# A hybrid attention and gMLP layer: the last gates are projected first, and q, k and the gMLP's constants take their pool

## The chip, the cores and the metric

The kernel runs on one core of one Trainium2 chip. The core has TensorE (PE, matrix products, with weight loads of its own, PEld), VectorE (DVE), ScalarE (ACT), GpSimd (POOL) and SyncE (SP), whose queue issues every transfer of this kernel. The metric is device time in microseconds of one execution; a time is the median of several runs. A profiled execution gives the trace from which the rows come; times in it count from the first instruction.

## What is computed

One decoder layer on 2048 tokens of width 1024, 8 heads of 64, a gMLP of width 512 in 4 groups, in float32 to the accuracy of the reference:

```python
a = _rmsnorm(h, g_in[i])
z = jnp.einsum('bsd,de->bse', a, w_in[i])
q, k, v, gate_b, u_a, v_a, gate_a = jnp.split(z, ...)          # seven groups of 512 columns
q = _rope(_rmsnorm(q, q_norm[i]), positions); k = _rope(_rmsnorm(k, k_norm[i]), positions)
o_b = _dilated_attention(q, k, v) * jax.nn.silu(gate_b)         # windows (128,1), (512,4), (2048,16)
o_a = _gmlp_spatial(u_a, v_a, w_spatial[i], b_spatial[i], ...) * jax.nn.silu(gate_a)
h = h + jnp.einsum('bse,ed->bsd', jnp.concatenate([o_b, o_a], axis=-1), w_out[i])
gate = jax.nn.sigmoid(jnp.einsum('bsd,de->bse', _rmsnorm(h, g_ple[i]), w_ple_gate[i]) + b_ple_gate[i])
h = h + gate * jnp.einsum('bsp,pd->bsd', p[i], w_ple_proj[i])
```

Each of the three dilated branches is causal attention of a query over 128 keys back at its stride; the branches are merged with weights in proportion to their softmax denominators. `_gmlp_spatial` is `gelu(u)` times a lower-triangular 128x128 mix of `LN(gelu(v))` in each chunk of 128 tokens.

## The kernel before

Tokens go in 16 tiles of 128. Every product of the layer is made of three float32r products of split operands (hi x hi, hi x lo, lo x hi; `project`, line 222, and `gm_product`, line 614): 24 matmuls of 512 columns. A group of 512 columns of weights is loaded in eight pieces of 256 KB into staging buffers (`stage()`, line 239, a pool of four), cast by ScalarE to the hi half (line 132), and VectorE or GpSimd subtracts for the lo half (line 134). It lies in a slot; three slots (`ring`) are used in turn, and the gate's group has one of its own in the pool `p1g`.

The work has three stages.

*Projection* (lines 268 to 539). For each tile the normalised row block is turned (`prep`), and four products g, q, k, v are made (`step`). q and k get norm and rotary embedding, are split into f16 halves, turned by a transposing transfer and stored (`d_qk`); v goes to `d_v` in two orders of tokens, the gate to `d_gb`. Everything on SP is in order. The last two tiles, 14 and 15, are done at the end, in the written order of PE (`manual_schedule`, line 529): q14 q15 k14 k15 v14 v15, then g14 g15 (lines 532 to 539). The pool `p1` is closed ahead of the gates, and the pool `pg` opens there, into which `gm_constants` (line 455) loads five constants of the gMLP, `bs` among them. `spatial_weights` (line 464) masks and turns the spatial matrices and scales `bs`; it is called in the first gate product of the gMLP (line 655).

*Attention and gMLP* (lines 598 to 841). Heads go in four pairs; a pair has three branches (0, 2, 1) of four quads of query tiles. A step (`Step`) makes scores for one or two tiles of both heads. `scores` (line 739): PE multiplies, VectorE adds the mask and takes the negated maximum into `o` (line 750), ScalarE takes the exponential (line 755). `turn` (line 758), one step later: ScalarE scales by 2^14 (line 762), VectorE casts to f16 (line 763), GpSimd subtracts for the lo half (line 113), and SP issues a transposing transfer (line 767; line 771 for narrow steps) out of a staging buffer of the pool of four. `values` (line 773), six steps after the scores: PE multiplies the turned tile with v (line 781), VectorE copies (line 787), and a finished quad of `o` is stored to `d_o` (line 790). There are 152 steps. Between them, `fill` puts gMLP products of the first 13 tiles into PE's written order, `FILL` = 1.3 us after each step and `BLOCK0` = 18 us ahead of the first; `gmlp` counts 0.43 us for two matmuls. The gMLP's own chain is the same for each tile: `gm_v`, `gm_u`, `gm_g`, GELU in `gelu2` (line 604), products in the two banks `mm`. q and k of a head pair lie in `qk`, and the next pair's are loaded in four chunks of 512 tokens over the last two quads of a pair and the first two of the next (`load_qk`, line 256, and lines 824 to 828), six transfers each; `load_v` (line 718) loads values two quads ahead.

*Output* (lines 844 to 926). The last three gMLP tiles (`tail`), then for each tile the merge of the branches (`mixed`, line 569, `merge`, line 542), output projection, norm and the per-layer gate.

The order of PE in the switch and in the attention loop is written; that of the other engines comes from a planner that works with its own costs. All tiles, loads and waits between engines follow from the order in which the program names them and from which pool's memory they take.

## Time and profile before

| | us |
|---|---|
| median of 3 runs | 1290.39 (1289.22 to 1294.34) |
| profiled execution | 1290.34 |
| its span, first to last instruction | 1288.4 |
| PE busy | 1203.9 (93%) |
| DVE busy | 893.7 (69%) |
| ACT busy | 654.0 (51%) |
| POOL busy | 511.2 (40%) |

Busy time is that of the whole span, and stages have different limits, so the rows below go by stretches. "Idle before" names the engine or transfer that ended a wait; where several ended together it is the last. A line can be that of a helper (line 226 is every `project`, line 113 every GpSimd product of `pool_tt`). PEclk is the granted clock of TensorE as a share of full speed.

### The profile page before, as it was taken

What the parts mean: (1) busy time and instruction counts of PE and PEld (TensorE: products, weight loads), DVE (VectorE), ACT (ScalarE), POOL (GpSimd) and SP (SyncE); (2) the same over time, 40 slices, a digit from 0 to 9 for tenths busy, and PEclk for the clock granted to TensorE, in tenths of its full rate; (3) what the DMA queues carried; (4) which work ended last, traced back from release to release, by engine and by line L of the source; (5) the groups of instructions that cost most, each with busy time, mean ns of one, the idle gap of its engine ahead of it and who ended that gap; (6) DMA issues with size and microseconds to landing.
All of it is one profiled execution on the core that took longest, in us unless ns stands there. A gap on an engine that the chain in (4) does not pass through costs nothing.

```text
span 1288.4 us, 21182 instructions
## 1 busy us (share of the span) xinstructions
PE 1203.9 (93%) x7166; PEld 972.6 (75%) x7166; DVE 893.7 (69%) x2253; ACT 654.0 (51%) x1273; POOL 511.2 (40%) x454
## 2 busy tenths in 40 slices
PE   5999999999994999899899899979999999999998
PEld 4778877778883787687687677768778888888886
DVE  5885565656575788688688778598766766666733
ACT  5754344344344687677677676344344344334322
POOL 4853343433462466565566565343121121121100
PEclk9999999999997999999999999989999999999999
DMA  7598777777668899999999999955546646645531
GB/s 265 159 229 199 163 189 168 166 181 175 170 175 238 202 202 233 211 230 233 208 226 233 210 228 211 232 157 183 148 115 155 175 118 154 168 117 139 133 89 49
DMA packets 456876, 233.19 MB, mean 181 GB/s; under 512 B 337472, under 2 KB 413888, under 8 KB 456768
## 3 DMA queue, kind: packets, MB, share of 16 engines
q1 hardware_dynamic: 456768, 231.85, 76.1%
q8 instruction: 56, 0.92, 0.3%
q14 instruction: 52, 0.43, 0.1%
HBM read 102.66 MB, written 57.28 MB: 124 GB/s over the span
## 4 chain that ended last, share of the span: by engine, by line
PE 34%; DMA 8%; DVE 6%; POOL 2%; issue 2%; ACT 2%; SPq 1%; DVEq 0%; POOLq 0%; ACTq 0%
PE mm L226 18%; PE gt L226 6%; PE mm L620 5%; DMA pt<-raw 4%; PE s L226 3%; DVE wslot L134 1%; PE pt L781 1%; PE s L747 1%; DMA d_o<-ost 1%; DVE pr L750 1%; DMA raw<-w_ple_gate 1%; POOL raw L113 1%; PE av L747 1%; DVE ob L558 1%; DVE raw L763 1%
## 5 line engine op out<-in xcount | busy, mean ns | idle before, releaser
L226 PE MATMUL mm<-wslot,aT 128*128 128x512 f32 x1536 | 365.5, 393 | 5.8 <-ACT wslot L132 3.3
L226 PEld LDWEIGHTS mm<-wslot,aT 128*128 128x128 f32 x1536 | 288.8, 188 | 72.0 <-ACT wslot L132 4.4
L620 PE MATMUL mm<-wslot,aT 128*128 128x512 f32 x1152 | 314.3, 414 | 24.3 <-DVE raw L611 16.6
L620 PEld LDWEIGHTS mm<-wslot,aT 128*128 128x128 f32 x1152 | 211.6, 195 | 63.8 <-DVE raw L611 17.1
L113 POOL TENSOR_TENSOR raw<-pr,raw 128x512 f16<-128x512 f32 (+1 forms) x152 | 176.6, 1163 | 154.4 <-DVE raw L763 122.1
L755 ACT ACTIVATE pr<-pr,ost 128x256 f32<-128x256 f32 (+1 forms) x384 | 153.6, 452 | 95.2 <-DVE ost L750 90.4
L226 PE MATMUL gt<-wslot,aT 128*128 128x512 f32 x744 | 179.1, 395 | 2.6 <-DVE gb L450 2.0
L226 PEld LDWEIGHTS gt<-wslot,aT 128*128 128x128 f32 x744 | 139.9, 189 | 35.9 <-DVE gb L450 3.2
L763 DVE CAST raw<-pr 128x512 f16<-128x512 f32 (+1 forms) x152 | 83.0, 548 | 52.5 <-DMA pt<-raw 43.8
L781 PEld LDWEIGHTS <-pt 128*128 128x128 f16 x1800 | 65.2, 98 | 62.8 <-DMA pt<-raw 31.7
L781 PE MATMUL pt<-sv,pt 128*128 128x65 f16 x1800 | 81.9, 195 | 21.9 <-DMA pt<-raw 20.6
L762 ACT ACTIVATE pr<-pr 128x512 f32<-128x512 f32 (+1 forms) x152 | 94.6, 623 | 3.5
L226 PE MATMUL av<-wslot,aT 128*128 128x512 f32 x360 | 87.6, 397 | 6.8 <-DVE gb L450 5.7
L226 PE MATMUL s<-wslot,aT 128*128 128x512 f32 x384 | 89.9, 389 | 1.5 <-POOL wslot L134 1.5
L750 DVE CUSTOM_DVE_ANT_0 pr<-s,mask 128x256 f32<-128x256 f32 (+1 forms) x256 | 80.6, 358 | 9.3 <-PE s L747 3.5
L113 POOL TENSOR_TENSOR m<-m,m 128x512 f32<-128x512 f32 x32 | 47.9, 1497 | 98.4 <-DVE rsh L146 92.5
L226 PEld LDWEIGHTS av<-wslot,aT 128*128 128x128 f32 x360 | 68.4, 191 | 23.6 <-DVE gb L450 7.4
L226 PEld LDWEIGHTS s<-wslot,aT 128*128 128x128 f32 x384 | 72.0, 188 | 16.8 <-POOL wslot L134 1.9
L747 PEld LDWEIGHTS <-sq 128*128 128x128 f16 x768 | 69.8, 120 | 11.2 <-DMA sk<-d_k 5.6
L560 POOL TENSOR_TENSOR ob<-ob 128x512 f32<-128x512 f32 x16 | 21.9, 1366 | 138.2 <-DVE ob L558 138.2
L747 PE MATMUL s<-sk,sq 128*128 128x256 f16 (+1 forms) x512 | 73.1, 276 | 3.6 <-DMA sk<-d_k 3.4
L563 POOL TENSOR_TENSOR ma<-ob,ma 128x512 f32<-128x512 f32 x16 | 22.2, 1385 | 126.4 <-DMA ma<-d_gb 91.2
(209 smaller groups left out, 1722.0 us busy)
## 6 DMA issues: line engine op xcount, KB each, us to landing
xt<-x SPq DMA_DIRECT2D x32, 512.0 KB, 4.5
d_o<-ost SPq DMA_DIRECT2D x48, 264.0 KB, 3.9
ob<-d_o SPq DMA_DIRECT2D x16, 792.0 KB, 5.3
raw<-w_in SPq DMA_DIRECT2D x38, 256.0 KB, 3.6
sv<-d_vt SPq DMA_DIRECT2D x32, 264.0 KB, 3.9
xt<-d_at SPq DMA_DIRECT2D x16, 512.0 KB, 4.4
sk<-d_k SPq DMA_DIRECT2D x64, 128.0 KB, 3.4
out<-th SPq DMA_DIRECT2D x32, 256.0 KB, 2.9
```

Source lines behind the costliest of these rows:

```text
L113: nc.gpsimd.tensor_tensor(dst, a, b, op=op)
L134: (nc.vector if dve else nc.gpsimd).tensor_tensor(lo, raw[:, i], hi.bitcast(F32), op=OP.subtract)
L226: nc.tensor.matmul(ps, aT[:, ha, k, :], w(slot, hw, k), start=(n == 0), stop=(n == 3 * nk - 1))
L560: nc.gpsimd.tensor_tensor(o, o, nums[:, 4:8], op=OP.add)
L563: nc.gpsimd.tensor_tensor(m, o, m, op=OP.mult)
L620: nc.tensor.matmul(ps, GT[c][:, ha, k, :], slots[g][:, hw, k, :], start=(n == 0), stop=(n == 23))
L747: nc.tensor.matmul(ps[:, c:c + nk], cols(br, j, Q[h]), cols(br, j, K, n, h, self.nb), start=(n == 0), stop=(n == 1))
L750: nc.vector.tensor_tensor_reduce(pr[:, c:c + nk], ps[:, c:c + nk], mask[:, m - nk:m], -1.0, 3e38, op0=OP.add, op1=OP.min, accum_out=o[:, j ...
L755: nc.scalar.activation(pr[:, c:c + nk], pr[:, c:c + nk], AF.Exp, bias=o[:, j - j0, 130 + h:131 + h], scale=-1.0)
L762: nc.scalar.activation(pr[:, :width], pr[:, :width], AF.Copy, scale=PSCALE)
L763: nc.vector.tensor_copy(ph, pr[:, :width])
L781: nc.tensor.matmul(PO[0][:, j % 2, h], self.pt[:, t, c // 128], vt[:, h, vv, 0:65], start=(n == 0), stop=(n == 3 * self.nb - 1))
```

## The change

- *The switch.* The last two gates are projected first, then q, k and v of the two tiles. `p1g` lies on the other side of memory, is closed behind the gates, and `pg` and the pool `p2` of q, k and the exponentials take its place. `gm_constants` comes directly behind, chunks 0 to 2 of q and k behind the q products, the spatial weights between k14 and k15, each group of gMLP weights behind the products that leave its slot. `gm_rows(0)` stands between v14 and v15, since tile 14's buffer is used for it. Chunk 3 is loaded ahead of the loop. `BLOCK0` is 6 instead of 18.
- *Scaled exponential.* VectorE adds log 2^14 to the negated maximum in `o` ahead of the exponential; ScalarE's scaling copy becomes the cast to f16, and VectorE's cast is gone. Denominator and numerator carry the same factor as before, and the merge uses differences of the maxima.
- *Wider packets.* `d_v` in the order for strided branches is stored by head pair, so that four tokens lie together for a load; `d_o` of branch 0 has four tokens together too, and `mixed` loads it by its own transfer; chunks 2 and 3 of q and k of the next head pair are one load, in keys that lie along one row.
- *Alike addresses.* Padding and numbers of small buffers; the first gMLP tile uses the pool `pg` like the others.

```diff
-BLOCK0, FILL = 18, 1.3
+BLOCK0, FILL = 6, 1.3
...
-    d_v = [dram.tile([S, HEADS, 2, 66], F16, name="d_v" + n) for n in "pt"]
+    d_vp = dram.tile([S, HEADS * 132], F16, name="d_vp")
+    d_vt = dram.tile([4, S, 264], F16, name="d_vt")
...
+    rawp.tile([128, 56], F32, name="pad", bufs=1)
...
-    def load_qk(qk, hp, c):
+    def load_qk(qk, hp, c, n=1):
-        tl = slice(512 * c, 512 * c + 512)
+        tl = slice(512 * c, 512 * (c + n))
...
-                nc.sync.dma_start(qk[1][i:i + 64, c, t], d_qk[1][64 * t:64 * t + 64, 2 * hp:2 * hp + 2, tl])
+                nc.sync.dma_start(qk[1][i:i + 64, t, :, tl], d_qk[1][64 * t:64 * t + 64, 2 * hp:2 * hp + 2, tl])
...
-        p1g = s1.enter_context(tc.tile_pool(name="p1g", bufs=1))
+        p1g = s1.enter_context(tc.tile_pool(name="p1g", bufs=1, side="right"))
...
-            nc.sync.dma_start(d_v[1][n * 128:(n + 1) * 128], vt)
-            nc.sync.dma_start(scattered(d_v[0][n * 128:], HEADS * 132, ((1, 32), (32, 4))), vt)
+            nc.sync.dma_start(d_vt[:, n * 128:(n + 1) * 128].rearrange("q p e -> p q e"),
+                              vt.rearrange("p (q h) t d -> p q (h t d)", h=2))
+            nc.sync.dma_start(scattered(d_vp[n * 128:], HEADS * 132, ((1, 32), (32, 4))), vt)
...
-                nc.vector.scalar_tensor_tensor(w, w, 0.25, keep, op0=OP.mult, op1=OP.mult)
+                last = nc.vector.scalar_tensor_tensor(w, w, 0.25, keep, op0=OP.mult, op1=OP.mult)
...
-            nc.vector.tensor_scalar(bs, bs, 0.25, None, op0=OP.mult)
+            with tc.issue_after(last.ins):
+                nc.vector.tensor_scalar(bs, bs, 0.25, None, op0=OP.mult)
...
-                AT[n] = norm_T(xt, xt, p1g if n % 3 == 2 else stream, turned, gbc)
+                AT[n] = norm_T(xt, xt, p1g if n % 3 == 1 else stream, turned, gbc)
...
+        for n in (NT - 2, NT - 1):
+            step(n, "g")
+        s1.close()
+        pg = gating.enter_context(tc.tile_pool(name="pg", bufs=1, side="right"))
+        p2 = s2.enter_context(tc.tile_pool(name="p2", bufs=1, side="right"))
+        qk = ([p2.tile([128, S], F16, name="sq" + n) for n in "01"],
+              p2.tile([128, 2, 2, S], F16, name="sk"))
+        gm_constants()
         XT[0] = load_x(d_at[0])
+
+        def load_gm(g, c):
+            slots[g] = load_group(w_in, 512 * c, new_slot(), stage, WD2)
+
+        for n in (NT - 2, NT - 1):
+            step(n, "q")
+        load_gm("va", 5)
+        for q in range(3):
+            for _ in load_qk(qk, 0, q):
+                pass
+        step(NT - 2, "k")
+        spatial_weights()
+        step(NT - 1, "k")
+        load_gm("ua", 4)
+        step(NT - 2, "v")
         gm_rows(0, stream)
-        for g in "qkv":
-            for n in (NT - 2, NT - 1):
-                step(n, g)
+        step(NT - 1, "v")
         s1q.close()
-        pg = gating.enter_context(tc.tile_pool(name="pg", bufs=1, side="right"))
-        gm_constants()
-        step(NT - 2, "g")
-        step(NT - 1, "g")
+        load_gm("ga", 6)
...
-        nc.sync.dma_start(ob, d_o[:, rows].rearrange("b p e -> p b e"))
+        near = d_o[0, n // 4 * 512 + n % 4:]
+        nc.sync.dma_start(ob[:, 0:4], bass.AP(tensor=near.tensor, offset=near.offset,
+                                              ap=[[4 * OW, 128], [S * OW, 4], [1, OW]]))
+        nc.sync.dma_start(ob[:, 4:12], d_o[4:12, rows].rearrange("b p e -> p b e"))
...
-            t = pool.tile([128, 512], F32, name=name, bufs=n) if c else stage()
+            t = pool.tile([128, 512], F32, name=name, bufs=n)
...
-            if c == 0:
-                spatial_weights()
...
-        for c, g in ((5, "va"), (4, "ua"), (6, "ga")):
-            slots[g] = load_group(w_in, 512 * c, new_slot(), stage, WD2)
...
-            rows = d_v[br > 0][:, 2 * hp:2 * hp + 2]
-            nc.sync.dma_start(t, tile_rows(rows, HEADS * 132, 264, br, j0, 4))
+            if br:
+                rows = tile_rows(d_vt[hp], 264, br, j0)
+            else:
+                a = d_vp[128 * j0:, 264 * hp:]
+                rows = bass.AP(tensor=a.tensor, offset=a.offset,
+                               ap=[[HEADS * 132, 128], [128 * HEADS * 132, 4], [1, 264]])
+            nc.sync.dma_start(t, rows)
...
+                nm = o[:, self.js[0] - j0:self.js[-1] + 1 - j0, 130:132]
+                nc.vector.tensor_scalar(nm, nm, math.log(PSCALE), None, op0=OP.add)
...
-                nc.scalar.activation(pr[:, :width], pr[:, :width], AF.Copy, scale=PSCALE)
-                nc.vector.tensor_copy(ph, pr[:, :width])
+                nc.scalar.activation(ph, pr[:, :width], AF.Copy)
...
-            for q in range(4):
-                for _ in load_qk(qk, 0, q):
-                    pass
-                if q < 2:
-                    hp, br, j0 = quads[q]
-                    load_v(br, hp, j0)
+            for q in range(2):
+                hp, br, j0 = quads[q]
+                load_v(br, hp, j0)
+            for _ in load_qk(qk, 0, 3):
+                pass
...
-                        h, c = {10: (1, 0), 11: (1, 1), 0: (0, 2), 1: (0, 3)}.get(i % 12, (4, 0))
-                        loads = load_qk(qk, hp + h, c) if i > 1 and hp + h < 4 else iter(())
+                        h, c = {10: (1, 0), 11: (1, 1), 0: (0, 2)}.get(i % 12, (4, 0))
+                        loads = load_qk(qk, hp + h, c, 1 + c // 2) if i > 1 and hp + h < 4 else iter(())
```

Left out: the pool `p2b` for values, turned tiles and `o` (before part of `p2`), the stores of `o` with four tokens together in branch 0 (`tile_rows`), the simpler addresses of keys in `cols`, and numbers of small buffers (`w`, `wd`, `mv`, `gple`).

## Rows read from the trace of the kernel before

**Rows 1.** Busy time by stage: stretch, us, then each engine, granted clock, DMA, GB/s.

```profile
60.00:341.50 281.50, 272.78 (x1186) 222.44 (x1185) 173.49 (x322) 120.37 (x201) 114.36 (x117) 0.99 0.76 182
...
396.00:424.30 28.30, 10.78 (x46) 8.59 (x46) 15.59 (x26) 10.07 (x17) 6.39 (x6) 0.70 0.78 232
...
424.30:804.00 379.70, 354.02 (x3405) 282.87 (x3405) 305.38 (x1170) 274.03 (x605) 225.68 (x195) 0.99 1.07 219
...
512.00:545.00 33.00, 27.26 (x232) 20.51 (x232) 22.87 (x80) 20.80 (x43) 18.30 (x16) 0.95 1.02 205
...
612.00:640.00 28.00, 22.76 (x196) 16.85 (x194) 20.97 (x72) 17.50 (x36) 15.25 (x14) 0.94 0.99 212
...
709.00:745.00 36.00, 28.74 (x279) 21.75 (x279) 24.95 (x88) 23.13 (x47) 19.24 (x18) 1.00 1.01 207
...
804.00:946.00 142.00, 129.17 (x656) 104.26 (x654) 107.24 (x209) 58.89 (x111) 44.59 (x36) 0.95 0.61 169
...
946.00:1288.40 342.40, 338.05 (x1463) 274.97 (x1461) 211.74 (x396) 127.54 (x230) 52.64 (x47) 1.00 0.52 131
```

**Rows 2.** Timeline of PE at the switch: start us, us, engine, line, idle before.

```profile
384.98 11.04 PE L620 MATMUL mm<-wslot,aT 128*128 128x512 f32 x48
...
412.66 7.48 PE L620 MATMUL mm<-wslot,aT 128*128 128x512 f32 x24 [16.64 <-DVE raw L611]
...
439.43 0.54 PE L781 MATMUL pt<-sv,pt 128*128 128x65 f16 x12 [1.26 <-DMA pt<-raw]
```

**Rows 3.** Timeline at the switch of ACT, SP and DVE, and SP's first q loads.

```profile
362.15 2.19 ACT L132 ACTIVATE wslot<-raw 128x512 fp32r<-128x512 f32 x4
...
404.85 0.63 ACT L132 ACTIVATE wslot<-raw 128x512 fp32r<-128x512 f32 x1
...
405.39 0.58 ACT L608 ACTIVATE raw<-mm 128x512 f32<-128x512 f32 x1
...
403.64 0.33 SPq L462 DMA_DIRECT2D lng<-ln_v_g  x1
...
410.47 0.17 DVE L476 TENSOR_SCALAR bs<-bs 128x4 f32<-128x4 f32 x1 [3.52 <-DMA bs<-b_spatial]
...
411.92 0.69 DVE L611 SCALAR_TENSOR_TENSOR raw<-raw,mm 128x512 f32<-128x512 f32 x1 [0.70 <-ACT raw L610]
...
413.12 0.80 SPq L260 DMA_DIRECT2D sq<-d_q  x2
```

**Rows 4.** Timeline of PE, one steady attention step, from values to values.

```profile
450.44 0.54 PE L781 MATMUL pt<-sv,pt 128*128 128x65 f16 x12
...
452.66 0.54 PE L781 MATMUL pt<-sv,pt 128*128 128x65 f16 x12
```

**Rows 5.** Timeline of SP and PE at the first change of head pair.

```profile
516.26 1.26 SPq L264 DMA_DIRECT2D sk<-d_k  x2
...
517.64 1.26 SPq L767 DMA_TRANSPOSE pt<-raw  x1
...
536.46 0.82 PE L747 MATMUL s<-sk,sq 128*128 128x256 f16 x3 [1.28 <-DMA sk<-d_k]
```

**Rows 6.** Groups of instructions in the attention stage, 424.3 to 804 us.

```profile
L113 POOL TENSOR_TENSOR raw<-pr,raw 128x512 f16<-128x512 f32 (+1 forms) x147 | 170.8, 1162 | 149.8 <-DVE raw L763 117.5 <-DVE mv L635 10.4 <-DVE rsl L146 6.6
...
L762 ACT ACTIVATE pr<-pr 128x512 f32<-128x512 f32 (+1 forms) x148 | 92.1, 623 | 3.4
...
L763 DVE CAST raw<-pr 128x512 f16<-128x512 f32 (+1 forms) x147 | 80.7, 550 | 52.3 <-DMA pt<-raw 43.8 <-ACT pr L755 2.3 <-ACT aT L192 2.1
```

**Rows 7.** A small scaling on DVE (ns, least/median/most); timeline of another beside POOL.

```profile
L146 DVE TENSOR_SCALAR rsh<-ssh x32: 158/278/1268, 47.3 to 383.6; 128x8 f32<-128x8 f32 x32
...
22.56 4.08 POOL L134 TENSOR_TENSOR wslot<-m,wslot 128x512 fp32r<-128x512 f32 x2
...
25.41 1.25 DVE L340 TENSOR_SCALAR lv_f<-lv_f 128x2 f32<-128x2 f32 x1
```

**Rows 8.** Timeline of PE among the last values.

```profile
807.95 0.54 PE L781 MATMUL pt<-sv,pt 128*128 128x65 f16 x12 [2.16 <-DMA pt<-raw]
```

More of the change, by code (lines that the diff above doesn't have):

```diff
@@ L598, in hybrid_layer @@
     with s2:
-        p2 = s2.enter_context(tc.tile_pool(name="p2", bufs=1))
+        p2b = s2.enter_context(tc.tile_pool(name="p2b", bufs=1))
         lng, lnb, mask = (CG[n] for n in ("lng", "lnb", "mask"))
@@ L633, in gm_v @@
             nc.vector.bn_stats(st, t)
-            mv = small.tile([128, 2], F32, name="mv")
+            mv = small.tile([128, 2], F32, name="mv", bufs=2)
             nc.vector.bn_aggr(mv, st)
@@ L690, in cols @@
                 return t[:, t0:t0 + 127 * st + 1:st]
-            def at(c):
-                return c // 512 * 2048 + c % 512
             if br == 0:
-                start, back, dims = at(128 * j), at(128 * (j - 1)), [[1, 128]]
+                start, back, dims = 128 * j, 128, [[1, 128]]
             elif br == 1:
-                start, dims = j // 4 * 2048 + 32 * (j % 4), [[128, 4], [1, 32]]
-                back = start - 2048
+                start, back, dims = j // 4 * 512 + 32 * (j % 4), 512, [[128, 4], [1, 32]]
             else:
-                start, dims = 32 * (j % 4) + j // 4, [[2048, 4], [128, 4], [4, 8]]
+                start, back, dims = 32 * (j % 4) + j // 4, 0, [[128, 16], [4, 8]]
             if blocks == 2:
-                start, dims = back, [[start - back, 2]] + dims
-            a = t[:, 0, part, h]
+                start, dims = start - back, [[back, 2]] + dims
+            a = t[:, part, h]
             return bass.AP(tensor=a.tensor, offset=a.offset + start, ap=[list(a.ap[0])] + dims)
@@ L805, in hybrid_layer @@
         steps = []
-        qk = ([p2.tile([128, S], F16, name="sq" + n) for n in "01"],
-              p2.tile([128, 4, 2, 2, 512], F16, name="sk"))
         loads = iter(())
         with in_order:
-            for q in range(4):
-                for _ in load_qk(qk, 0, q):
-                    pass
-                if q < 2:
-                    hp, br, j0 = quads[q]
-                    load_v(br, hp, j0)
+            for q in range(2):
[3 more added lines that the diff above has]
+                pass
             for n in range(len(plan) + LAG_C):
@@ L849, in hybrid_layer @@
         wo, wg = [], []
-        gple = pm.tile([128, 32], F32, name="gple")[:, 0:8]
+        gple = pm.tile([128, 64], F32, name="gple")[:, 0:8]
         nc.sync.dma_start(gple, io["g_ple"].rearrange("o (k p) -> p (o k)", p=128))
```

17 lines of the change are left out of this document (8 added, 9 removed).

## The prediction

> **What bounds the kernel now.** I read the table by stage first [rows 1]. In the output stage (946 us to the end) TensorE is busy 338 of 342 us, and in the attention stage (424 to 804) 354 of 380: TensorE is the bound nearly everywhere, so an edit saves time only where TensorE stands still or at half clock. There are three such places. The stretch from 396 to 424, where projection gives way to the gMLP and attention, has 10.8 us of work in 28.3, at a mean granted clock of 0.70. The three changes of head pair (512 to 545, 612 to 640, 709 to 745) lack 5.7, 5.2 and 7.3 us. And 804 to 946, from the last attention steps into the output stage, lacks 12.8.
>
> The chain of waits around the first place says why. TensorE ended the first two gMLP products at 396.0 and stood 16.64 us for a bank of `mm` [rows 2]. The releaser is the GELU of the first product (line 611), which ran at 411.92 [rows 3]. Its Square (line 608) stood on ScalarE behind the casts of 24 pieces of gMLP weights, the first at 362.15 and the last at 404.85, and ran at 405.39. Then VectorE, in order, was held until 410.47 by the little scaling of `bs`, whose load could only start at 403.64, when the projection's pool was free [rows 3]. So three things in a row: weights, a pool that is freed late, a load that VectorE waits for. When TensorE came back, its clock was at half level: the 24 matmuls from 412.66 took 7.48 us, where 48 took 11.04 before [rows 2], so 7.48 - 5.52 = 1.96 us more. With the first wait for a transposed tile, 1.26 us at 439.43 [rows 2], the place costs 16.64 + 1.96 + 1.26 = 19.9 us.
>
> **Part by part: the switch.** The order of the last eight projections becomes g14 g15 q14 q15 k14 k15 v14 v15, and the gate's pool ends after the second of them. TensorE's work is the same; with no new stall it still comes to the gMLP at 385. What moves: the five constants and three of four chunks of q and k are loaded some 40 us earlier (the gate now ends at 385 - 6 x 5.5 = 352), and `bs` is scaled behind the masks, so VectorE isn't held by it alone. The fill ahead of the first attention step goes from 18 to 6 us, so the first gate product no longer follows the second product directly: after one product (5.5 us, half of 11.04) and four matmuls come attention steps, about five until the rest of that second product is through. A step takes 2.2 us in steady state (450.44 to 452.66 [rows 4]) and some 0.4 less while there are no values yet. So the gate product, first to need the bank on which TensorE stood, starts near 385 + 5.5 + 1 + 5 x 1.8 = 400.
>
> What is late next: the gate's weights. 24 casts took 362.15 to 405.5, 1.8 us each; then, the four staging buffers set that pace and not the slots. The slots now come free at 363, 374 and 385 (four, two and no projections of 5.5 us ahead of the end), about as fast as the pieces come. So the last piece again comes near 406. The SP queue now has 18 loads of q and k among the pieces, 0.40 us each for q and 0.63 for k [rows 3, 5]: 6 x 0.40 + 12 x 0.63 = 10 us of issue, which delays the last piece by 0 to 10 us. The gate product reads its eight pieces in order, so it wants the last hi piece at some 402. Also the first attention steps take their staging buffers behind those pieces, so their transposed tiles land near 408, for values due at 404. The two waits overlap. I take 6 us for both (1 us where the ten us of issue are hidden, 14 us where none is), nearer to the lower end, since the two overlap. Net: -19.9 + 6 = -13.9, between -19 and -6.
>
> Costed at nothing: the four transposes of the spatial weights, now between k14 and k15 in TensorE's written order. Behind them are k15, both v and the gMLP. Their cover is three projections, 16.5 us; the loads they need took 6.8 us from first issue to the wait's end (403.64 to 410.47 [rows 3]), after a gate epilogue and its store. If that cover is gone, TensorE stands for the rest. Also `gm_rows(0)`, which now waits for tile 14's buffer: v15 covers it with 5.5 us.
>
> **The attention steps.** Of each of 152 steps the VectorE cast goes (550 ns mean, 80.7 us [rows 6]), ScalarE's scaling copy (623 ns) becomes the cast, and VectorE gets an add on 2 or 4 values between mask and exponential. The add has no row of its own. The nearest are two scalings: of 8 values, 158 ns at least and 1268 at most, and of 2 values, which began at 25.41 beside a GpSimd instruction and ended with it, at 26.65 [rows 7]. GpSimd is busy 225.7 of 379.7 us of this stage [rows 1]; a wait of half a subtraction (1162 ns [rows 6]) in 59% of cases gives 0.16 + 0.59 x 0.58 = 0.5 us. VectorE then has 305.4 - 80.7 + 152 x 0.5 = 301 us, as much as before, and stays beside TensorE's 354. I take 0; if the add always waits it is a rival, below.
>
> The Trainium skill ("SBUF — State Buffer", section "SBUF: two separate sides") says that VectorE and GpSimd share a port pair as an exclusive lock, on which a VectorE op in a two-port mode waits for the whole GpSimd instruction. The trace agrees (1.25 us for two values). By that rule the removed cast frees GpSimd, and each new add is exposed to it.
>
> The wait for a staging buffer moves from VectorE to ScalarE with the cast; ScalarE is busy 274 of 380 us and has room. The SP queue issues the same transposes.
>
> **The changes of head pair.** Here the SP queue is the limit: a quad of four steps lasts 4 x 2.2 = 8.9 us, and it has four transposes of 1.26 and six loads of q and k, 2 x 0.40 + 4 x 0.63 [rows 3, 5], 8.4 us in all before any value load, store of `o` or gMLP transfer. That keys come late shows on TensorE too (1.28 us at 536.46 for `sk` [rows 5]). The change makes the last two of four chunks one: six issues fewer, 6 of 24, in the fourth quad of each change; the other three quads stay overfull. A quarter of 18.2 us of idle time is 4.5; I take -4, between 0 and -13 (if the backlog of the fourth quad was most of it).
>
> **Moved to the end.** 12 us of gMLP product go from ahead of the steps to behind them. Before, gMLP tails filled TensorE between the last values, and it stood 2.16 us [rows 8]. Now the rest of the loop's gMLP stands in the written order behind the last values, and five steps of values have no fill: at worst TensorE stands for five fills of six matmuls, 5 x 6 x 0.23 = 7 us. Against it, that rest covers the way of the last store of `o` to the merge, in a stretch that lacks 12.8 us [rows 1]. I take +2, between -5 and +7.
>
> **Nothing.** One more load of `ob` per tile falls in the output stage, narrower stores of `v` in the projection (TensorE busy 272.8 of 281.5 us [rows 1]), and TensorE is covered in both. Wider loads of values and stores of `o` are ones that TensorE doesn't wait for in the loop. Tile addresses and padding have nothing in the trace to price them; 0 for each, and what shorter queues might give the transposes is in the first rival.
>
> **The sum** goes against the profiled execution, 1290.34 us (span 1288.4 and 1.94 around it; the median of the runs is 1290.39): -13.9 - 4 + 2 = -15.9, so 1274.
>
> **The rivals.** (1) *More goes:* the switch keeps 2 us of stall, and the shorter way of a step (no hop to VectorE) with less queueing empties most of the head-pair idle time: -18 - 13 + 0, 1259. For: VectorE stood 43.8 us of the stage for a staging buffer [rows 6]. Against: SP, not VectorE, holds the tiles there. (2) *The wait comes back at the switch:* the Square again stands behind the late casts, TensorE waits from 400 to 414 or so: -6 - 4 + 2, 1282. For: ScalarE's order was the first link of the old wait. Against: attention steps now stand between. (3) *It doesn't do what it says:* q, k and constants are issued behind the weights and come no earlier, the end costs 5 and the other terms bring 5 to 9: 1286 to 1290. Against: their addresses are free 40 us earlier. (4) *Slower:* the add waits for GpSimd in every step, 1.25 us. VectorE then has 224.7 + 152 x 1.25 = 415 us in a stage of 380, and it becomes the bound: +35, less 12 from the other terms, 1313. It decides from a mean add of (380 - 225)/152 = 1.0 us. For: the scaling of two values lost just that. Against: GpSimd is free 41% of the time.
>
> **How the numbers follow.** Forecast 0.58 (1264 to 1283, the terms' bounds joined as independent ones), (1) 0.15, (2) 0.12, (3) 0.06, (4) 0.09. A measurement of this kernel tells 0.5%, 6.5 us, from no change: below 1283.9 is faster. Faster: nearly all of the forecast, (1) and part of (2), 0.76; within 0.5%: the rest of (2) and (3), 0.15; slower: (4), 0.09. The range reaches from below (1) to (3): 1256 to 1288.
>
> **What would show it.** Right: between the end of the projections and the first values no TensorE wait over 6 us and full clock; no wait of VectorE for `bs`; the fourth quad after a change of head pair without idle time, the first three as before; adds of 0.2 to 0.8 us. Wrong: a wait for `wslot` or the GELU near 400, a mean add over 1 us with VectorE above 95% in the steps, or idle time behind the last values over 7 us.

## The result, and the profile after

Timed in turns with the kernel before, the changed kernel takes 1301.17 us (median) against 1292.54: a ratio of 1.0067, 95% interval 1.0051 to 1.0083. It is slower by 0.7%, about 8.7 us, where 1274 was forecast, in a range of 1256 to 1288. Its profiled execution took 1296.61 us, the least of its 15, span 1294.8, so 6.4 us more span than before.

Where did it go? First the table by stage of the changed kernel (stretch, its length, busy time of TensorE, its weight loads, VectorE, ScalarE and GpSimd, then granted clock, DMA share, GB/s):

```profile
60.00:341.50 281.50, 271.71 (x1186) 221.48 (x1185) 173.67 (x323) 121.08 (x201) 115.75 (x117) 1.00 0.77 182
341.50:424.30 82.80, 57.32 (x252) 46.56 (x252) 48.04 (x82) 30.93 (x52) 33.97 (x25) 0.88 0.83 209
424.30:804.00 379.70, 356.93 (x3433) 286.01 (x3433) 294.68 (x1180) 272.19 (x614) 229.46 (x197) 0.98 1.04 220
804.00:946.00 142.00, 126.26 (x615) 101.44 (x615) 98.45 (x186) 51.06 (x98) 42.67 (x33) 0.95 0.56 160
946.00:1294.80 348.80, 342.40 (x1510) 282.96 (x1508) 221.82 (x411) 133.85 (x242) 57.57 (x50) 1.00 0.49 131
```

Read each row as length less TensorE's busy time, beside [rows 1]. At the switch TensorE now stands 25.5 us. Before, it worked until 396.0 [rows 2] and stood 28.3 - 10.8 = 17.5, so the switch that was to win 14 us loses 8. The attention stage stands 22.8 us against 25.7, a gain of 2.9. From 804 to 946 it stands 15.7 against 12.8, and in the output stage 6.4 against 4.4. From 60 us on that is 11 us more idle time for 6.4 us of span; the rest is TensorE's busy time, which is 1203.9 us on the page of before and 1198.9 on this one, where ends of matmuls are modelled.

Now the switch, on the timeline of TensorE (start, length, what ended the idle time before it):

```profile
352.66 11.04 PE L227 MATMUL mm<-wslot,aT 128*128 128x512 f32 x48
363.54 5.60 PE L227 MATMUL s<-wslot,aT 128*128 128x512 f32 x24
389.80 1.09 PE L477 MATMUL pt<-ident,gg 128*128 128x128 f32 x4 [20.66 <-DVE gg L476]
390.54 7.36 PE L227 MATMUL s<-wslot,aT 128*128 128x512 f32 x24
...
414.97 0.40 PE L770 MATMUL av<-sk,sq 128*128 128x128 f16 x4
...
424.31 0.64 PE L770 MATMUL av<-sk,sq 128*128 128x256 f16 x4 [4.82 <-DVE ost L773]
```

After k of tile 14 TensorE stands 20.66 us at the four transposes of the spatial weights, with k15, v14 and v15 behind them in its written order, though their operands are there. The first projection afterwards begins at half clock, 7.36 us against 5.60: the granted clock was 0.50 from 380 to 390 us and 0.80 from 390 to 400. The old wait for the bank [rows 2] is gone; this one is longer. A second of 4.82 us follows in the first attention steps.

Who is late? The same stretch on SyncE, ScalarE and VectorE, followed backwards:

```profile
389.42 0.89 DVE L476 SCALAR_TENSOR_TENSOR gg<-gg,raw 128x128 f32<-128x128 f32 x4
...
383.79 0.69 DVE L135 TENSOR_TENSOR wslot<-raw,wslot 128x512 fp32r<-128x512 f32 x1 [6.71 <-ACT wslot L133]
...
383.13 0.63 ACT L133 ACTIVATE wslot<-raw 128x512 fp32r<-128x512 f32 x1 [10.19 <-DMA raw<-w_in]
...
378.68 0.53 SPq L127 DMA_DIRECT2D raw<-w_in  x1
...
370.37 0.98 SPq L262 DMA_DIRECT2D sq<-d_q  x2
371.39 3.14 SPq L266 DMA_DIRECT2D sk<-d_k  x4
...
367.79 0.33 SPq L465 DMA_DIRECT2D lng<-ln_v_g  x1
...
364.34 0.60 ACT L452 ACTIVATE gb<-pt 128x512 f32<-128x512 f32 x1 [3.18 <-DMA d_gb<-gb]
```

VectorE scaled the spatial weights at 389.42, in order behind the low half of the fifth gMLP weight piece, for which it stood 6.71 us, and of 5 us of its other work. ScalarE had stood 10.19 us for that piece's load. SyncE issued it at 378.68, behind 12 loads of q and k and the constants, and the constants had waited for the gate's pool: both last gates share one buffer, so the second gate's tanh stood 3.18 us for the first one's store, and the constants were issued at 367.79. They are early, as the change meant (403.64 before [rows 3]); what they are needed for is not.

The gMLP's weights are the other thing to look at. One row tells their 24 casts on ScalarE (ns least/median/most, first and last start):

```profile
L133 ACT ACTIVATE wslot<-raw x24: 614/629/635, 366.8 to 423.8; 128x512 fp32r<-128x512 f32 x24
```

Before, they ran from 362.15 to 404.85 [rows 3]. They start 4.7 us later and end 19 us later. Part of that is the wait itself: the slots of k and v came free only with k15 and v15, at 397.9 and 408.8, and the 9th and the 17th cast began at 398.66 and 409.40.

The last values, which had one wait of 2.16 us [rows 8]:

```profile
809.06 0.54 PE L806 MATMUL pt<-sv,pt 128*128 128x65 f16 x12 [2.82 <-DMA pt<-raw]
810.01 0.54 PE L806 MATMUL pt<-sv,pt 128*128 128x65 f16 x12 [0.41 <-DMA pt<-raw]
811.15 0.84 PE L806 MATMUL pt<-sv,pt 128*128 128x65 f16 x12 [0.60 <-DMA pt<-raw]
816.50 0.84 PE L806 MATMUL pt<-sv,pt 128*128 128x65 f16 x12 [4.51 <-DMA pt<-raw]
```

That is 8.3 us. What is left of the gMLP stands behind them in the written order, and nothing between them. It is not all loss: before, TensorE stood a little later instead, for the GELU (4.76 us at 847.90). Up to the first product of the output stage, in the kernel before and in the changed one, the stretch behind 804 us stands 9.9 and 12.2 us:

```profile
804.00:878.27 74.27, 64.41 (x371) 52.50 (x368) 56.05 (x107) 30.98 (x58) 29.17 (x24) 0.91 0.73 200
...
804.00:887.03 83.03, 70.81 (x375) 57.23 (x374) 54.04 (x100) 29.84 (x56) 27.34 (x23) 0.94 0.60 168
```

### The profile page after: what moved, and what is told of

It reads as the page before. It is cut to its first block, busy times and chain, and to the rows that moved or that the text cites. A ratio compares the mean times of both kernels' runs of the same rounds, so it can differ in the third digit from the quotient of the medians.

```text
span 1294.8 us, 21315 instructions
## 1 busy us (share of the span) xinstructions
PE 1198.9 (93%) x7166; PEld 972.6 (75%) x7166; DVE 878.0 (68%) x2253; ACT 647.6 (50%) x1273; POOL 516.2 (40%) x454
## 4 chain that ended last, share of the span: by engine, by line
PE 40%; DMA 21%; DVE 14%; issue 7%; ACT 7%; POOL 6%; SPq 4%; DVEq 0%; ACTq 0%; POOLq 0%
PE mm L227 17%; PE mm L646 8%; PE gt L227 5%; DMA pt<-raw 4%; DMA st<-hl 4%; PE s L227 3%; DMA xt<-raw 3%; PE s L770 2%; PE pt L806 2%; DMA sk<-d_k 2%; ACT raw L179 2%; DVE aT L194 2%; DVE pr L773 2%; DVE m L421 1%; POOL rsh L148 1%
## 5 line engine op out<-in xcount | busy, mean ns | idle before, releaser
L781 ACT ACTIVATE pr<-pr,ost 128x256 f32<-128x256 f32 (+1 forms) x384 | 150.3, 451 | 67.4 <-DVE ost L779 66.3
L788 ACT ACTIVATE raw<-pr 128x512 f16<-128x512 f32 (+1 forms) x152 | 93.0, 619 | 34.9 <-DMA pt<-raw 32.9
L227 PEld LDWEIGHTS s<-wslot,aT 128*128 128x128 f32 x384 | 73.2, 191 | 17.2 <-POOL wslot L135 1.8
L227 PEld LDWEIGHTS av<-wslot,aT 128*128 128x128 f32 x360 | 67.5, 189 | 22.8 <-DVE gb L453 7.0
L770 PEld LDWEIGHTS <-sq 128*128 128x128 f16 x768 | 70.3, 121 | 16.7 <-issue 12.8
L779 DVE TENSOR_SCALAR ost<-ost 128x2 f32<-128x2 f32 (+1 forms) x152 | 63.1, 417 | 2.3
```

The lines of the kernel that those rows point to most:

```text
L227: nc.tensor.matmul(ps, aT[:, ha, k, :], w(slot, hw, k), start=(n == 0), stop=(n == 3 * nk - 1))
L770: nc.tensor.matmul(ps[:, c:c + nk], cols(br, j, Q[h]), cols(br, j, K, n, h, self.nb), start=(n == 0), stop=(n == 1))
L779: nc.vector.tensor_scalar(nm, nm, math.log(PSCALE), None, op0=OP.add)
L781: nc.scalar.activation(pr[:, c:c + nk], pr[:, c:c + nk], AF.Exp, bias=o[:, j - j0, 130 + h:131 + h], scale=-1.0)
L788: nc.scalar.activation(ph, pr[:, :width], AF.Copy)
```

## The experiments

Ratios are to the kernel before, timed in turns with each, with 95% intervals; the changed kernel has 1.0067. The four times are starts of the 1st, 8th, 16th and 24th cast of gMLP weights on ScalarE.

| run | kernel | ratio | casts, us |
|---|---|---|---|
| | before | 1 | 362 375 391 405 |
| | changed | 1.0067 [1.0051, 1.0083] | 367 386 407 424 |
| e10 | changed, whole order undone | 0.9984 [0.9967, 1.0001] | 363 376 391 408 |
| e12 | the same, exponential undone too | 0.9983 [0.9966, 1.0001] | 364 377 392 408 |
| e16 | e10 with the gate first | 1.0027 [1.0008, 1.0046] | 367 387 405 421 |
| e3 | changed, BLOCK0 18 | 1.0019 [0.9997, 1.0042] | 367 386 408 423 |
| e15 | before, BLOCK0 6 | 1.0181 [1.0153, 1.0209] | 362 375 390 405 |
| e1 | changed, transposes late | 1.0073 [1.0046, 1.0100] | 370 388 408 425 |
| e7 | changed, q and k behind va | 1.0084 [1.0066, 1.0103] | 368 381 413 430 |
| e14 | e1 and e7 together | 1.0125 [1.0099, 1.0150] | 369 382 415 432 |
| e9 | changed, q first | 1.0065 [1.0045, 1.0085] | 362 375 420 437 |
| e11 | q first, e7, BLOCK0 18, transposes behind v14 | 1.0040 [1.0025, 1.0056] | 365 378 412 430 |
| e13 | e11 with e1's late transposes | 1.0064 [1.0039, 1.0089] | 364 377 410 431 |
| e17 | changed, wide q and k loads | 1.0072 [1.0053, 1.0092] | 369 392 414 429 |
| e4 | before, scaled exponential alone | 1.0053 [1.0031, 1.0074] | |
| e5 | changed, exponential undone | 1.0068 [1.0051, 1.0085] | |
| e8 | e3 and e5 together | 1.0035 [1.0022, 1.0047] | |

**Which part loses: the exponential, or the order?** First the exponential alone in the kernel before (e4):

```diff
+ nm = o[:, self.js[0] - j0:self.js[-1] + 1 - j0, 130:132]
+ nc.vector.tensor_scalar(nm, nm, math.log(PSCALE), None, op0=OP.add)
...
- nc.scalar.activation(pr[:, :width], pr[:, :width], AF.Copy, scale=PSCALE)
- nc.vector.tensor_copy(ph, pr[:, :width])
+ nc.scalar.activation(ph, pr[:, :width], AF.Copy)
```

> The kernel before with one part of the change alone: log(PSCALE) is added to the norms on VectorE ahead of each step's exponentials, ScalarE writes the fp16 copy itself, and VectorE's cast is gone. Theory (the step's cost is nothing, as predicted: 152 adds of about 0.42 us for 152 casts on an engine that has slack): within 4 us of the kernel before, ratio 0.997 to 1.003. Rival (the add waits for GpSimd's lock of the port in each step, the fourth rival of the prediction): 10 us or more slower, ratio above 1.008.

It was 0.5% slower. Its groups on ScalarE in the attention stage show the wait for a staging buffer that the prediction moved there, 40.2 us (VectorE's was 43.8 [rows 6]):

```profile
L764 ACT ACTIVATE raw<-pr 128x512 f16<-128x512 f32 (+1 forms) x148 | 91.0, 620 | 42.3 <-DMA pt<-raw 40.2
```

So the next theory was that this wait costs the time, and e5 took the same part out of the changed kernel:

> The changed kernel without its scaled exponential: no add on the norms, ScalarE scales the probabilities in place, and VectorE makes the fp16 copy, as in the kernel before. Theory (from the run in which the kernel before got the scaled exponential alone and became 0.5% slower: the fp16 copy writes the staging buffer, so ScalarE, and no longer VectorE, is the engine that stands still until the transposing DMA has freed one; 37 us of such idle time stood on ScalarE in its attention steps, 39 us on VectorE in the kernel before): the time falls by 4 to 9 us, to a ratio of 0.999 to 1.003, and ScalarE's waits for the transposing DMA go back to under 5 us. Rival (the loss of that run belongs to the kernel before alone, or the loss of the changed kernel is at the switch and the end only): within 3 us of the changed kernel, ratio 1.005 to 1.009.

The rival held: 1.0068, no difference, though ScalarE's waits for the transposing DMA went. Then the order was undone whole and the rest kept (e10), and the exponential undone on top (e12):

```diff
+ XT[0] = load_x(d_at[0])
+ gm_rows(0, stream)
+ for g in "qkv":
+     for n in (NT - 2, NT - 1):
+         step(n, g)
+ s1q.close()
  for n in (NT - 2, NT - 1):
      step(n, "g")
  s1.close()
...
  gm_constants()
- XT[0] = load_x(d_at[0])
...
- for n in (NT - 2, NT - 1):
-     step(n, "q")
  load_gm("va", 5)
+ load_gm("ua", 4)
+ load_gm("ga", 6)
  for q in range(3):
      for _ in load_qk(qk, 0, q):
          pass
- step(NT - 2, "k")
- spatial_weights()
...
```

The steps that follow go too, the transposes return to `gm_g`, and BLOCK0 is 18.

> The changed kernel with its whole new order at the switch undone: q, k, v, then the gate, constants and q and k loads behind the projections, the transposes in the gating of gMLP tile 0, BLOCK0 18; the scaled exponential, the wider packets and the addresses stay. Theory (the order is the whole of the loss; the rest is worth nothing): the switch has one wait of 15 to 18 us as in the kernel before; ratio 0.998 to 1.004. Rival (the other parts cost the loss, as the scaled exponential alone did in the kernel before): ratio 1.005 or more.

> As the run with the whole order undone, and the scaled exponential undone too: what is left of the change is the wider packets and the addresses. Theory (packets and addresses cost nothing, as predicted): ratio 0.997 to 1.003. Rival (packets or addresses cost part of the loss): 1.004 or more. The difference to the run with the order undone is the price of the scaled exponential in that order: 0.5% by the run on the kernel before, nothing by the run on the changed kernel.

0.9984 and 0.9983: without the order the change is level with the kernel before, or just ahead of it. At the switch e10 stands 17.2 us, as the kernel before (17.5). In this order neither the exponential nor packets and addresses together have a price that can be measured. That e4 alone lost 0.5% stays unexplained: its attention stage stands no longer (24.4 us against 25.7), and taken out of the changed kernel (e5), of e3 (e8) or of e10 (e12) the same edit gives nothing back.

**What in the order: BLOCK0.** One number, in each of the two orders:

> The changed kernel with one number: BLOCK0 is 18, as in the kernel before, in place of 6, so that fewer gMLP steps are taken into the first attention steps and more are left over for the last ones. Theory (the small BLOCK0 has spent the gMLP steps that filled TensorE at the end of the attention loop): the idle time of TensorE behind the last scores, 8.3 us in the changed kernel, falls to 2 to 4 us and its half clock there goes; the start of the loop gains at most 4 us of waits; the time falls by 2 to 6 us. Rival (the end follows from the order of the loads and not from the count of leftover steps): the idle time there stays at 7 us or more, and the time within 2 us or above.

> The kernel before with one number: BLOCK0 is 6 in place of 18. Theory (BLOCK0 alone is about half of the loss, whatever the order at the switch): the idle time behind the last scores rises from 2.2 to 6 to 9 us, and the first attention steps wait 1 to 4 us more; ratio 1.003 to 1.007. Rival (in the old order the smaller BLOCK0 takes the wait of 16.6 us for the bank away, as predicted, and wins more than the end loses): ratio below 0.998.

> The changed kernel with two edits: BLOCK0 is 18 as before, and the scaled exponential is undone. Theory (the two losses are separate and add up: about 7 us by BLOCK0, about 7 us by the wait that moved to ScalarE): ratio 0.994 to 0.999, so faster than the kernel before by 2 to 7 us. Rival (the two share a cause, both the lateness of what fills TensorE at the end of the loop): no better than BLOCK0 = 18 alone, ratio 1.000 to 1.004.

In the new order 18 brings the time from 1.0067 to 1.0019, some 6 us. With the exponential undone too (e8) it is 1.0035, so there was nothing to add up. The values at the end stand 0.94 us at most, 2.3 in all, and follow each other with gMLP products between:

```profile
811.11 0.54 PE L806 MATMUL pt<-sv,pt 128*128 128x65 f16 x12 [0.94 <-DMA pt<-raw]
812.11 0.54 PE L806 MATMUL pt<-sv,pt 128*128 128x65 f16 x12 [0.46 <-DMA pt<-raw]
812.48 5.03 PE L646 MATMUL mm<-wslot,aT 128*128 128x512 f32 x21
...
850.88 13.51 PE L646 MATMUL mm<-wslot,aT 128*128 128x512 f32 x48 [6.43 <-DVE gv L637]
```

But a wait for the GELU, 6.43 us, is back a little later, as before. The stages of e3 (the last up to the first product of the output stage) tell where the 6 us lie:

```profile
341.50:424.30 82.80, 61.04 (x259) 49.49 (x258) 47.98 (x78) 31.90 (x53) 34.56 (x26) 0.88 0.82 212
...
424.30:804.00 379.70, 357.88 (x3408) 287.17 (x3407) 304.32 (x1172) 269.60 (x606) 225.21 (x195) 0.98 1.03 217
...
804.00:880.03 76.03, 64.65 (x399) 52.67 (x397) 55.95 (x111) 32.32 (x61) 27.39 (x24) 0.96 0.72 192
```

TensorE stands 21.8, 21.8 and 11.4 us, in the changed kernel 25.5, 22.8 and 12.2. So most of the gain lies at the switch, where the first scores no longer wait 4.82 us, and little at the end.

In the old order 6 costs 1.8%, far more than expected: the first scores come up before q and k, which stand there behind the weights and the constants.

```profile
418.26 0.86 PE L747 MATMUL av<-sk,sq 128*128 128x128 f16 x4 [27.21 <-DMA sk<-d_k]
```

So early q and k are what a BLOCK0 of 6 needs. With 18, in the kernel before, the first scores did not wait for them.

**What in the order: the longest wait?** e1 writes the four transposes where the kernel before has them; e7 holds q and k back.

```diff
  step(NT - 2, "k")
- spatial_weights()
  step(NT - 1, "k")
...
  pool_tt(t, t, G["u", c], OP.mult)
+ if c == 0:
+     spatial_weights()
```

> The changed kernel with one edit: the four TensorE transposes of the spatial weights are written where the kernel before has them, in the gating of gMLP tile 0, and no longer between the two k projections of tiles 14 and 15. Theory (the place in TensorE's written order is the cause: the projections k15, v14 and v15, which need nothing late, stand behind transposes whose constants and mask come late): the wait of 20.7 us ahead of L477 goes, the half clock of 373 to 394 us with it, and the three projections run by about 380 us; the time falls by 12 to 20 us, to 1277 to 1285, so 0.990 +- 0.004 of the kernel before. First rival (the gMLP weights behind the q and k loads are the cause wherever the transposes stand): TensorE then waits about as long, for the casts of the gMLP weights ahead of the first gMLP product, or VectorE's evictions of the projections stand behind the casts; the time stays within 4 us of the changed kernel's. Second rival (the loss lies in the attention steps or at the end): the wait goes and the time falls by under 6 us.

The 20.7 us went from the transposes, and the time stayed (1.0073). TensorE waits elsewhere instead, at the gMLP, the scores and again the transposes:

```profile
399.84 9.46 PE L645 MATMUL mm<-wslot,aT 128*128 128x512 f32 x28 [11.66 <-ACT aT L193]
...
419.63 1.01 PE L771 MATMUL av<-sk,sq 128*128 128x256 f16 x4 [5.96 <-DVE ost L774]
...
436.61 0.47 PE L477 MATMUL pt<-ident,gg 128*128 128x128 f32 x1 [3.61 <-DVE gg L476]
```

Writing the q and k loads later in the text changed nothing to speak of (e2, 1.0073 [1.0050, 1.0096]): SyncE's order is the planner's, and 12 of 18 still stood ahead of the fifth piece. An ordering edge behind the last load of the va weights, `WL[0]`, held them back:

```diff
+ with tc.issue_after(WL[0].ins):
      for q in range(3):
          for _ in load_qk(qk, 0, q):
              pass
```

> The changed kernel with the three chunks of q and k loads held on SyncE's queue behind the eighth load of the va weights by an ordering edge; the earlier attempt to write them later had left 12 of 18 ahead of the fifth weight piece, since SyncE's order is the planner's and not that of the text. Theory (the weights stand behind the q and k loads, VectorE's in-order queue stands behind the weights' cast, and the scaling of the spatial weights stands behind that): the fifth piece is issued at about 373 us instead of 378.7, the cast of its low half comes at 379 to 381 instead of 383.8, and the wait ahead of L477 falls from 20.7 to 13 to 16 us; the time falls by 4 to 9 us. Rival (the four staging buffers come free no earlier, since VectorE and GpSimd still cast pieces 1 to 4 till 378 us): the fifth piece is issued at 376 us or later, the wait stays above 18 us and the time within 3 us.

The local half of the theory came true: piece five was issued at 373.03 and cast at 376.46, and the transposes waited 11.12 us, less than expected. The time did not follow (1.0084), for TensorE then waited for the next weights, whose loads now stood behind q and k, eight times and 8.3 us in all, of which two:

```profile
381.44 0.66 PE L479 MATMUL pt<-ident,gg 128*128 128x128 f32 x2 [11.12 <-DVE gg L478]
...
411.21 0.80 PE L649 MATMUL mm<-wslot,aT 128*128 128x512 f32 x1 [2.72 <-ACT wslot L135]
...
429.46 0.79 PE L649 MATMUL mm<-wslot,aT 128*128 128x512 f32 x1 [1.66 <-ACT wslot L135]
```

Did each hide the other? Both edits together (e14):

> The changed kernel with the two edits that each left the time as it was, together: the transposes in the gating of gMLP tile 0, and q and k held behind the va weights on SyncE. BLOCK0 stays 6. Theory (one wait hid behind the other): no wait over 6 us between the projections and the first scores; the time falls by 5 to 10 us, ratio 0.999 to 1.003. Rival (the third and fourth groups of weights and the fill are what TensorE waits for in the end): ratio 1.005 to 1.010, with the waits behind the first scores, at the ua and ga weights.

Worse, 1.0125. Many waits for weights took the place of the one, 6.98 us the longest, and the clock was lower: 0.83 on the mean from 340 to 450 us against 0.89 in the changed kernel.

Third, the one gate buffer (e6): the gate of tile 15 takes one of the two buffers of the q and k norms.

```diff
- g = p1g.tile([128, 512], F32, name="gb")
+ g = p1g.tile([128, 512], F32, name="gb") if n < NT - 1 else (
+     p1.tile([128, HEADS, 2, 32], F32, name="m1", bufs=2).rearrange("p h t c -> p (h t c)"))
```

> The changed kernel with the gate of tile 15 in a buffer of its own (one of the two m1 buffers of the q and k norms) in place of the one gate buffer. Theory (two gates behind each other and one buffer make the whole chain late: ScalarE waited 3.2 us for the store of gate 14 with the gMLP's first four weight casts queued behind it, and the pool of the gate went to the constants only when the store of gate 15 had been read): ScalarE's second gate follows the first within 1 us, the constants are issued 2 to 4 us earlier, the wait of 20.7 us ahead of L477 falls by 2 to 4 us; the time falls by 2 to 5 us. Rival (SyncE's queue and the four staging buffers set the time of the weights anyway): the wait stays above 19.5 us and the time within 2 us.

1.0111 [1.0089, 1.0132], with a wait of 21.57 us ahead of the transposes: no help, and the norms' lost buffer may have cost something.

**What in the order: the gate's place?** The gMLP's first weights go into the slot of q's weights, so q first should let them in earlier (e9); e11 and e13 join this to the other edits.

```diff
- for n in (NT - 2, NT - 1):
-     step(n, "g")
+ for g in "qg":
+     for n in (NT - 2, NT - 1):
+         step(n, g)
...
- for n in (NT - 2, NT - 1):
-     step(n, "q")
```

> The changed kernel with one edit of order: the last two tiles' q goes first and their gate second (q14 q15 g14 g15 k14, transposes of the spatial weights, k15 v14 v15). Theory (putting the gate ahead of q holds back the slot of the q weights, which is the one that the gMLP's first weights go into: TensorE let go of it at 363 us in the changed kernel against 352.5 in the kernel before, and every later slot in turn; the casts of the gMLP weights began at 366.9 and ended at 423.8 us against 362.2 to 404.9): the first four casts come at 358 to 363 us, the wait ahead of L477 falls from 20.7 to 8 to 14 us and the last cast comes before 416 us; the time falls by 6 to 14 us. Rival (the four staging buffers and SyncE's queue set the pace whatever slot is free; holding q and k back shortened the wait by 9.5 us and the time came out the same): the last cast stays behind 420 us and the time within 4 us of the changed kernel, ratio 1.004 to 1.010.

> The changed kernel with what the runs so far point to: q14 q15 g14 g15 k14 k15 v14, transposes of the spatial weights, v15; q and k loads held behind the va weights on SyncE; BLOCK0 18. Theory (earlier slots, weights ahead of q and k, and fill at the end add up): the switch has under 15 us of waits in all, the idle time behind the last scores is under 3 us; ratio 0.988 to 0.996, faster than the kernel before. Rival (the casts of 24 weight pieces through four staging buffers end near 415 to 420 us in any order, and what is taken from the first wait comes back in the later ones): ratio 0.998 to 1.004, about BLOCK0 18 alone.

> The changed kernel with q14 q15 g14 g15 k14 k15 v14 v15, the transposes of the spatial weights in the gating of gMLP tile 0, q and k loads held behind the va weights on SyncE, BLOCK0 18: the run that waited 27.8 us, with the transposes taken out of the projections. Theory (each wait at the switch hides another: with the constants late, since the gate is second, the transposes must be late too; then the early slots and the early weights show): no single wait over 10 us before the first values; ratio 0.990 to 0.998. Rival (the 24 weight pieces, 18 loads of q and k and the constants need the same 45 to 60 us on SyncE, ScalarE and the staging buffers in any order, and TensorE waits for their end): the waits at the switch add up to 17 us or more again; ratio 0.999 to 1.004.

The first eight casts came at the old times, 362 to 375. But the gate was second now. In e9 the constants were issued at 384.33, 16.5 us later, and the transposes stood 22.36 us, with VectorE waiting for the mask. In e11 the transposes stood 27.81 us, with VectorE once more behind a weight piece. With the transposes taken out of the projections (e13) the longest waits were 8.73 and 6.11 us, for weights. None beat BLOCK0 18 by itself. Last, the gate's place alone, on e10:

```diff
- for g in "qkv":
+ for g in "gqkv":
      for n in (NT - 2, NT - 1):
          step(n, g)
  s1q.close()
- for n in (NT - 2, NT - 1):
-     step(n, "g")
  s1.close()
```

> As the run with the whole order undone (0.9984), and one step of it done again: the gate of the last two tiles goes first, so its pool gives way early and the constants and q and k are issued early; the transposes stay in the gating of gMLP tile 0 and BLOCK0 stays 18. Theory (gate first is the other half of the loss: it holds back the slot of q by two projections and puts 12 to 18 loads of q and k ahead of the gMLP's weights on SyncE): TensorE's wait for the first gMLP weights is 8 to 14 us, the later casts end 10 to 18 us later; ratio 1.001 to 1.006. Rival (gate first is worth what was predicted, and only the transposes and BLOCK0 lost): ratio below 0.996.

0.9984 becomes 1.0027: the gate's place, with the early loads that come with it, costs 0.4%, some 5.5 us. The casts tell where: the first 4 us later (q, whose slot it takes, is projected behind two gates), the eighth 10 (constants, q and k in between), the sixteenth 14.

**Issues, or bytes?** With q and k chunks 0 to 2 as one, 6 loads replace 18 (e17):

```diff
- for q in range(3):
-     for _ in load_qk(qk, 0, q):
-         pass
+ for _ in load_qk(qk, 0, 0, 3):
+     pass
```

> The changed kernel with the first three chunks of q and k as one: 6 loads in place of 18 on SyncE at the switch, the same bytes. Theory (the orders tried so far all wait because the switch has more issues for SyncE and more casts than the projections cover, and an edit that only moves them moves the wait; fewer issues shorten it): 12 issues of some 0.6 us go, 7 us of SyncE; the fifth weight piece is issued at 373 to 375 us instead of 378.7, the wait ahead of L477 falls to 13 to 17 us, and the last gMLP cast comes 4 to 8 us before 423.8; the time falls by 3 to 8 us, ratio 1.000 to 1.005. Rival (the four staging buffers and the casts bound the weights, so the gain comes back as when q and k were held behind the weights): the last cast stays at 420 us or later, ratio 1.006 to 1.009.

The fifth piece was issued at 376.55, 2 us earlier, and yet cast 6 us later:

```profile
376.55 5.08 SPq L127 DMA_DIRECT2D raw<-w_in  x4
...
389.52 0.63 ACT L133 ACTIVATE wslot<-raw 128x512 fp32r<-128x512 f32 x1 [14.35 <-DMA raw<-w_in]
```

And the stretch from 380 to 390 us in the table of windows, columns as above:

```profile
380.00:390.00 10.00, 0.00 (x0) 0.00 (x0) 0.00 (x0) 0.48 (x1) 0.21 (x1) 0.50 1.10 229
```

TensorE computes nothing, and the DMA engines are full (share 1.10). Here it is the transfers put ahead, and not the number of issues, that hold the piece up: a piece lands 3.6 us after its issue in the kernel before (median from 360 to 425 us), here 13. The edit changed two things, though: all 18 loads' bytes (2.3 MB) now go ahead of that piece, and in the changed kernel 12 loads' (1.5 MB) did. There the piece was cast 4.5 us after its issue, so what came late there was the issue. The same edit in the old order:

> The run with the whole order undone (0.9984), with the first three chunks of q and k as one. Theory (there the loads of q and k stand behind the weights and the constants, and the first attention steps wait for nothing of them): no more than 2 us, ratio 0.996 to 1.000. Rival (SyncE's queue holds the first transposes and values of the attention loop behind those loads): 0.992 to 0.996.

It was worth nothing there (1.0008 [0.9991, 1.0024]).

The Trainium skill ("DMA: Bandwidth & Descriptors", section "Two DMAs through the same engine are not ordered") says that descriptors of one queue on one DMA engine start in order, though pipelined; the 13 us of that piece behind six wide loads agree.

## Why the prediction was wrong

Its terms were -13.9 (switch), -4 (head pairs), +2 (end), 0 (the rest); measured was +8.7.

- *The switch.* Three steps failed. The first is "The slots now come free at 363, 374 and 385 [...] So the last piece again comes near 406". It came at 423.8. The loads of q and k ahead of the pieces were priced by SyncE's issue, 10 us at most; the constants, and the gates' epilogues with their one buffer, which stand ahead of them too, had no price. e16 against e10 gives the place of the gate, with all that follows, 5.5 us of loss; and with a third of the issues (e17) the last cast comes at 429. The slots of k and v were late too, 398 and 409, by the wait itself; but in e1 they came free at 377 and 388, and the last cast stood at 425 all the same.
- The second is "Costed at nothing: the four transposes". The cover of "three projections, 16.5 us" was there: q14, q15 and k14 ran from the end of the gates, 352.7, to 369.1. (k15, v14 and v15 stand behind the transposes in TensorE's order and wait with them.) But it was set against 6.8 us of loads alone. The gate's epilogue and store, which the text names without a price, took until 367.79, when the first constant was issued; and the scaling that feeds the transposes was not followed into VectorE's queue, where it stood behind a weight cast and other work until 389.42. The text had the right conditional ("If that cover is gone, TensorE stands for the rest"), not its price, 20.7 us.
- The third is that a wait is worth its length ("the place costs 16.64 + 1.96 + 1.26 = 19.9 us"). The wait at 412 was taken away, as forecast, and 20.7 us stood ahead of 389.8; taken away there, 24 us stood in the five waits of e1 that are over 1 us. e7, e13 and e14 show the same. In each of these orders TensorE waited somewhere at the switch for weights, constants, or an engine that had them in its queue.
- *Moved to the end.* The term was right, +2: from 804 us to the output stage TensorE stands 12.2 us against 9.9. The sign of being wrong, "idle time behind the last values over 7 us", did read 8.3 among them, but waits for the GELU fell in exchange. What the text did not price is what BLOCK0 does at the switch: of the 6 us that e3 gives back, the larger part lies there.
- *The attention steps* at 0 fit e10 and e12, which agree within their intervals, and e5; e4, 0.5% slower, does not fit and stays open. The adds took 417 ns on the mean, 0.5 estimated:

```profile
L779 DVE TENSOR_SCALAR ost<-ost x152: 150/170/1250, 425.5 to 806.0; 128x2 f32<-128x2 f32 x112, 128x4 f32<-128x4 f32 x40
```

The median is 170 ns, the most 1250. The lock between VectorE and GpSimd that the Trainium skill states ("SBUF — State Buffer", section "SBUF: two separate sides") fits the longest: an add of 1.25 us, from 426.75, ended at 428.00, and a GpSimd instruction that had begun at 426.24 at 427.97. It spares most. Rival (4), the add that waits in every step, falls: the mean add is not the 1.0 us from which it decides, and VectorE is busy 294.7 of 379.7 us in that stage.
- *The changes of head pair* won nothing where they were looked for. In the three stretches of [rows 1] TensorE stands 33 - 27.6, 28 - 22.2 and 36 - 29.5, in all 17.7 us against 18.2. The stage as a whole stands 2.9 us less, near the 4 forecast, but not for the reason given; that nearness is luck.
- *Packets and addresses* at 0 were right, taken together (e12).
- *The rivals.* (2), the wait that comes back at the switch, was the nearest, but it came at another place and dearer than the 14 us that its 1282 us was made with. (1) falls with the head pairs, and (3) since q and k were issued from 370.37, before from 413.12. No rival had the new order itself as the loser; the one slower case was put on the adds.

What stays open is how the loss at the switch divides between transfers, the casts on three engines and the four staging buffers: every edit moved more than one of them, and no run changed the number of buffers.

## What to carry to other kernels

A long wait in a well covered kernel is often where a shortage of supply shows, and not what it costs: before it is taken away, list all that must be loaded and cast by then, and ask what stands next. A load that is issued earlier than it is needed is not free, since what is needed first stands behind its issue or its transfer. And an instruction that is moved in a written order is covered by the work ahead of it, never by that behind it.

## What the runs showed of the hardware

A busy DMA share says little of the rate: with six loads of 384 KB ahead the 16 engines were full at 229 GB/s (380 to 390 us of e17), and as full, 1.08, at 355 GB/s in e7:

```profile
410.00:420.00 10.00, 8.30 (x26) 5.32 (x27) 7.73 (x22) 5.18 (x9) 4.15 (x4) 0.66 1.08 355
```

After 20 us of idle time the granted clock stood at half level (0.50), and 24 matmuls took 7.36 us in place of 5.60. With several short waits (e14) the mean from 340 to 450 us was 0.83, with one long wait (the changed kernel) 0.89.
